# Two layers of a hybrid decoder trunk: weight and activation tiles moved to other SBUF addresses

## The chip, the core and the metric

The kernel runs on one core of one Trainium2 chip. The time is device microseconds of one execution, and the number compared is the median of three executions. The profile is of one further execution, and its records give the start and length of every instruction on TensorE (PE for its matmuls, PEld for its weight loads), VectorE (DVE), ScalarE (ACT), GpSimd (POOL) and of the DMA transfers that SyncE (SP) issues.

## What is computed

The reference is a decoder trunk with two layers over 256 tokens of width 1024, all in float32. Each layer is, cut to its matrix products:

```python
for i in range(DEPTH):                       # DEPTH = 2
    h = rms_norm(x, mix_norm_g[i])
    z = h @ w_in[i]                          # 1024 -> 4608: q, k, v, ssm, conv, three gates
    y_attn = sliding_window_attention(...) @ w_attn_out[i]
    y_ssm = glu(gelu(s5_ssm(...)) @ w_ssm_glu[i] + b_ssm_glu[i])
    y_conv = conformer_conv(...)             # ends in @ w_pw_out
    merged = gates[0] * y_attn + gates[1] * y_ssm + gates[2] * y_conv
    x = x + merged @ w_mix_out[i]
    f_gate, f_up = split(rms_norm(x, ffn_norm_g[i]) @ w_ffn_in[i])     # 1024 -> 2 x 2816
    x = x + (silu(f_gate) * f_up) @ w_ffn_out[i]
    e = p[i] @ w_ple_in[i]
    x = x + sigmoid(rms_norm(x, ple_norm_g[i]) @ w_ple_gate[i]) * e
return rms_norm(x, final_norm_g)
```

## The kernel before

All weights are read once from HBM, as 260 pairs of blocks of 128x512 floats (`total`, line 309). A pair lands in one of three `raw` tiles (`load_w`, line 313). ScalarE rounds it to a `wh` tile in the type float32r and VectorE writes the remainder into a `wl` tile (`split`, line 229, called from `prep_w`, line 336). There are four `wh` and four `wl` tiles, 4096 bytes per partition each, all from the pool `wp` (line 88). Activations are split in the same way into a high and a low tile, from the pool `act`: the groups `b4` (4096 bytes, line 92) and `b2` (2048 bytes, line 95).

`gemm` (line 462) forms a product as three float32r matmuls, high by high, high by low and low by high. The stationary operand is 128 columns of an activation tile (512 bytes per partition) and the moving operand is 512 columns of a weight tile (2048 bytes per partition):

```python
mm(acc[t], hi, wh[:, kk, :], k == 0, False)
mm(acc[t], hi, wl[:, kk, :], False, False)
mm(acc[t], lo, wh[:, kk, :], False, last)
```

One pair of blocks serves two token halves and two k, so 12 such matmuls. The last four pairs are the exception: `last_gate` (line 1369) uses them 512 columns wide for the first token half and in two parts of 256 columns for the second. Gate and GLU products end in a bias matmul whose moving operand is a `brow` tile and whose stationary operand is `sdT` (for gates, line 1161) or `ones` (for the GLU, line 1203): 24 and 16 of them. So there are 3,072 + 24 + 40 = 3,136 matmuls of 512 float32r columns in the products, and 12 more that write the attention mask. The last pair of weights has its split tiles in `b4` (lines 340 to 342, named `whl` and `wll`), not in `wp`.

The order of all instructions is written by hand: a planner in Python (`run`, line 122, `may_run`, line 403, `pump`, line 417) keeps a modelled clock per engine and decides after each half pair which piece of side work is emitted. For it, a 512-column float32r matmul costs 0.4167 ns a column plus `PE_SET`, 13.3 ns (lines 44 and 225). The planner keys its tiles by name and by offset inside the tile; it knows no SBUF address.

Tiles get their addresses in the order in which the pools are opened and in which each tile or tag is first asked for: first `cp` (constants, `x0`, `x1`, tables), then `wp` (`raw`, `wh`, `wl`), then `act`, which begins with the statistics tiles `nst` (128 bytes each, `norm_stats`, line 490) and goes on with `b4`, `b1`, the small tiles and `b2`. A tile that grows ahead of them therefore moves everything behind it.

Of the kernel before, what the change touches and what calls it, by code (L numbers as in the profile page):

```python
# [6 lines left out]
F32 = mybir.dt.float32  # L7
# [9 lines left out]
NT = 2  # L17
# [64 lines left out]
def trunk_kernel(tc, wts, par, bmat, cst_d, x_d, pos_d, pt_d, bias_d, fg_d, out_d, dbg=None):  # L82
# [3 lines left out]
    with ctx:  # L86
        cp = ctx.enter_context(tc.tile_pool(name="cp", bufs=1))
        wp = ctx.enter_context(tc.tile_pool(name="wp", bufs=5))
        act = ctx.enter_context(tc.tile_pool(name="act", bufs=2))
# [158 lines left out]
                dbg(nc, name, ap)  # L248

        cst = cp.tile([128, C_MASK], F32, name="cst")  # L250
        xs = [cp.tile([128, D], F32, name=f"x{t}") for t in range(NT)]
        pos = cp.tile([128, NT], I32, name="pos")
        pars = [cst[:, C_PAR:C_MASK], cp.tile([128, N_PA], F32, name="par1")]
# [234 lines left out]
                    pump(slack)  # L488

        def norm_stats():  # L490
            return act.tile([128, 16, NT], F32, tag="nst", bufs=5, name="nst")

        def stat(sts, i, t):
            return sts[:, i, t:t + 1]
# [601 lines left out]
        def layer(l, feat, sts, prep):  # L1096
# [156 lines left out]
            mT.upto(2)  # L1253

            fst = norm_stats()
            fT = []

# [52 lines left out]
            def hid_lhs(t, k):  # L1310
                while len(hid) <= k // 2:
                    push()
                return hid[k // 2][0][:, t, k % 2, :], hid[k // 2][1][:, t, k % 2, :]

            pst = norm_stats()
            gT = []
            for n in range(2):
# [16 lines left out]
            gT[0].upto(2)  # L1334

            nst = norm_stats()
            nT = []

# [311 lines left out]
```

## Time and profile before

| | before |
|---|---|
| median of three runs | 862.08 us (859.58 to 862.19) |
| the profiled execution's own time | 860.29 us |
| span of its profile | 858.5 us |
| mean granted TensorE clock | 0.994 |
| PE busy | 840.4 us, 98% |
| DVE, ACT, POOL busy | 68%, 53%, 15% |
| DMA | 141.34 MB, mean 165 GB/s |

Matmuls overlap in the records: one starts before the one ahead of it has ended. The length of a record is therefore no price. The step from one start to the next is, and so is the length of a piece of the chain divided by the matmuls in it.

### The profile page before, as it was taken

To read this page: it belongs to the slowest core of one execution; us is meant where nothing else is said; L and a number is where in the kernel's file an instruction comes from. 1 tells how busy PE (TensorE), PEld (TensorE's weight loads), DVE (VectorE), ACT (ScalarE), POOL (GpSimd) and SP (SyncE) were. 2 spreads that over 40 slices of the span, in tenths; PEclk is the share of its full clock that TensorE was granted. 3 is DMA by queue.
4 is the path that set the end of the run, shared out by engine and by line. 5 is a ranking of instruction groups with operands and counts; after the bars stand their busy time and mean duration, and the time that the engine had idled before them with its cause. 6 is when DMAs were issued, how large, how long until landed. Compare 5 with 4: busy or idle time off the path is not lost.

```text
span 858.5 us, 11139 instructions
## 1 busy us (share of the span) xinstructions
PE 840.4 (98%) x3976; PEld 686.8 (80%) x3976; DVE 580.9 (68%) x865; ACT 457.2 (53%) x745; POOL 126.8 (15%) x325
## 2 busy tenths in 40 slices
PE   8989999899999999999999999999999999999996
PEld 7877788688888888888888878878888888888885
DVE  4688875887667784654577599568766666654555
ACT  5675756345556666543564554544554454444454
POOL 5787001000744200000020000100000000000001
PEclk9999999989999999999999999999999999999999
DMA  7554533436765654666654443655566666666661
GB/s 252 181 178 138 152 120 98 123 99 180 211 173 177 187 177 148 179 182 190 184 152 145 124 123 101 191 174 173 172 185 180 182 177 187 181 179 189 182 185 75
DMA packets 41199, 141.34 MB, mean 165 GB/s; under 512 B 4756, under 2 KB 6404, under 8 KB 41144
## 3 DMA queue, kind: packets, MB, share of 16 engines
q1 hardware_dynamic: 41144, 140.64, 55.2%
q8 instruction: 31, 0.51, 0.2%
q14 instruction: 24, 0.20, 0.1%
HBM read 139.49 MB, written 1.13 MB: 164 GB/s over the span
## 4 chain that ended last, share of the span: by engine, by line
PE 88%; ACT 4%; DVE 3%; DMA 2%; POOL 1%; issue 1%; SPq 0%; POOLq 0%; ACTq 0%; DVEq 0%
PE fz L227 29%; PE g L227 15%; PE fo L227 14%; PE mo L227 5%; PE pz L227 4%; PE yg L227 3%; DMA raw<-in_wts 2%; PE ya L227 2%; PE sc L227 2%; PE pl L227 1%; PE zq L227 1%; PE ez L227 1%; PE zc L227 1%; PE yc L227 1%; PE yx L227 1%; ACT wh L176 1%
## 5 line engine op out<-in xcount | busy, mean ns | idle before, releaser
L200 DVE TENSOR_TENSOR wl<-raw,wh 128x1024 fp32r<-128x1024 f32 (+1 forms) x261 | 316.2, 1215 | 212.5 <-ACT wh L176 212.4
L176 ACT CAST wh<-raw 128x1024 fp32r<-128x1024 f32 (+1 forms) x261 | 271.6, 1043 | 205.2 <-PE fo L227 57.0
L200 POOL TENSOR_TENSOR nst<-nst 128x2 f32<-128x2 f32 (+1 forms) x14 | 2.8, 199 | 538.9 <-ACT sqj L171 538.4
L227 PE MATMUL fz<-wh,f0h 128*128 128x512 f32 x176 | 70.9, 403 | 0.0
L227 PE MATMUL fz<-wh,f1h 128*128 128x512 f32 x176 | 70.4, 400 | 0.0
L227 PE MATMUL fo<-wh,hdh 128*128 128x512 f32 x176 | 69.8, 397 | 0.0
L227 PE MATMUL fz<-wh,f1l 128*128 128x512 f32 x176 | 69.6, 395 | 0.0
L227 PE MATMUL fz<-wh,f0l 128*128 128x512 f32 x176 | 69.5, 395 | 0.0
L227 PE MATMUL fo<-wh,hdl 128*128 128x512 f32 x176 | 69.5, 395 | 0.0
L227 PE MATMUL fo<-wl,hdh 128*128 128x512 f32 x176 | 69.5, 395 | 0.0
L227 PE MATMUL fz<-wl,f1h 128*128 128x512 f32 x176 | 69.5, 395 | 0.0
L227 PE MATMUL fz<-wl,f0h 128*128 128x512 f32 x176 | 69.4, 394 | 0.0
L227 PEld LDWEIGHTS fo<-wh,hdl 128*128 128x128 f32 x176 | 33.1, 188 | 7.9
L227 PEld LDWEIGHTS fz<-wh,f1l 128*128 128x128 f32 x176 | 33.1, 188 | 7.9
L227 PEld LDWEIGHTS fz<-wh,f0l 128*128 128x128 f32 x176 | 33.1, 188 | 7.8
L227 PEld LDWEIGHTS fo<-wh,hdh 128*128 128x128 f32 x176 | 33.1, 188 | 7.7
L227 PE MATMUL g<-wh,h1h 128*128 128x512 f32 x96 | 38.7, 403 | 0.6 <-DVE M L210 0.6
L227 PEld LDWEIGHTS fo<-wl,hdh 128*128 128x128 f32 x176 | 33.1, 188 | 7.6
L227 PEld LDWEIGHTS fz<-wl,f1h 128*128 128x128 f32 x176 | 33.1, 188 | 7.5
L227 PEld LDWEIGHTS fz<-wh,f1h 128*128 128x128 f32 x176 | 33.1, 188 | 7.4
L227 PE MATMUL g<-wh,h0h 128*128 128x512 f32 x96 | 39.0, 406 | 0.0
L227 PEld LDWEIGHTS fz<-wl,f0h 128*128 128x128 f32 x176 | 33.2, 188 | 7.2
(390 smaller groups left out, 1766.6 us busy)
## 6 DMA issues: line engine op xcount, KB each, us to landing
raw<-in_wts SPq DMA_DIRECT2D x258, 512.0 KB
raw<-in_wts SPq DMA_DIRECT2D x4, 256.0 KB
out<-e SPq DMA_DIRECT2D x4, 256.0 KB
x<-in_x SPq DMA_DIRECT2D x4, 128.0 KB
x<-in_x SPq DMA_DIRECT2D x2, 256.0 KB
bm<-in_bmat SPq DMA_DIRECT2D x4, 128.0 KB
pT<-in_pt SPq DMA_DIRECT2D x2, 256.0 KB
fgb<-in_fg SPq DMA_DIRECT2D x1, 512.0 KB
```

The costliest lines, as they stand in the source:

```text
L176: ACT.copy(out=out, in_=in_)
L200: (eng or DVE).tensor_tensor(out=out, in0=a, in1=b, op=op)
L227: PE.matmul(out, lhsT, rhs, start=start, stop=stop)
```

## The change

One tile that nothing uses, of 40 floats (160 bytes), is asked for behind `cst`, and the statistics tiles are six instead of five (128 bytes more).

```diff
         cst = cp.tile([128, C_MASK], F32, name="cst")
+        cp.tile([128, 40], F32, name="pad")
         xs = [cp.tile([128, D], F32, name=f"x{t}") for t in range(NT)]
@@
         def norm_stats():
-            return act.tile([128, 16, NT], F32, tag="nst", bufs=5, name="nst")
+            return act.tile([128, 16, NT], F32, tag="nst", bufs=6, name="nst")
```

The instructions of every engine, their order and what they wait for stand as before; only addresses differ. Everything in `cp` behind `cst` and all of `wp` moves by 160 bytes, and everything in `act` behind `nst` by 288 bytes. The start within a partition, as the remainder by 1024 and by 512:

| tiles | mod 1024 before | after | mod 512 before | after |
|---|---|---|---|---|
| `raw`, `wh`, `wl` | 864 | 0 | 352 | 0 |
| `b4`, `b1`, `b2`: activations high and low, `whl`, `wll` | 480 or 992 | 256 or 768 | 480 | 256 |
| `x0`, `x1` | 704 | 864 | 192 | 352 |
| `brow` | 384 | 544 | 384 | 32 |
| `sdT` | 384 | 544 | 384 | 32 |
| `ones` | 384 | 32 | 384 | 32 |
| `cst` (with the identity of the transposes) | 128 | 128 | 128 | 128 |

Offsets inside a tile are multiples of 512 bytes for the stationary operands and of 2048 bytes for the moving ones (1024 in the parts of 256 columns), so the column by 512 holds for each operand that a matmul reads.

## Rows read from the trace of the kernel before

**Rows 1.** The page: busy time of the engines, and the granted clock.
```profile
PE 840.4 (98%) x3976; PEld 686.8 (80%) x3976; DVE 580.9 (68%) x865; ACT 457.2 (53%) x745; POOL 126.8 (15%) x325
...
PEclk9999999989999999999999999999999999999999
```
**Rows 2.** The page: the chain that ended last, by engine.
```profile
PE 88%; ACT 4%; DVE 3%; DMA 2%; POOL 1%; issue 1%; SPq 0%; POOLq 0%; ACTq 0%; DVEq 0%
```
**Rows 3.** What PE waited for: us in total, times, longest.
```profile
PE sT L307 <- DVE gtm L214: 3.2, 1, 3.2
PE h0p L307 <- DMA x<-in_x: 1.5, 2, 0.9
PE sc L227 <- ACT qT L171: 1.5, 1, 1.5
```
**Rows 4.** The chain in order of time: start us, us, what.
```profile
10.22 5.71 DMA raw<-in_wts
33.65 5.12 DMA raw<-in_wts
...
265.31 11.20 PE fz L227 x48
...
352.11 29.39 PE fo L227 x126
382.37 29.27 PE fo L227 x126
```
**Rows 5.** Busy time of each engine in three of those pieces.
```profile
265.31:276.51 11.20, 11.20 (x50) 8.97 (x50) 6.84 (x11) 10.14 (x15) 6.84 (x28) 1.00 0.56 172
352.11:381.50 29.39, 29.39 (x129) 23.62 (x128) 14.13 (x13) 12.20 (x15) 0.00 (x0) 1.00 0.63 184
```
**Rows 6.** PE in order of time, inside the first FFN product: start us, us.
```profile
303.07 0.39 PE L227 MATMUL fz<-wl,f0h 128*128 128x512 f32 x1
303.30 0.40 PE L227 MATMUL fz<-wh,f0l 128*128 128x512 f32 x1
303.54 0.39 PE L227 MATMUL fz<-wh,f0h 128*128 128x512 f32 x1
303.76 0.40 PE L227 MATMUL fz<-wl,f0h 128*128 128x512 f32 x1
304.00 0.39 PE L227 MATMUL fz<-wh,f0l 128*128 128x512 f32 x1
304.23 0.40 PE L227 MATMUL fz<-wh,f0h 128*128 128x512 f32 x1
304.47 0.39 PE L227 MATMUL fz<-wl,f0h 128*128 128x512 f32 x1
304.70 0.40 PE L227 MATMUL fz<-wh,f0l 128*128 128x512 f32 x1
304.94 0.39 PE L227 MATMUL fz<-wh,f0h 128*128 128x512 f32 x1
```
**Rows 7.** PEld in order of time, the same stretch.
```profile
303.07 0.19 PEld L227 LDWEIGHTS fz<-wh,f0l 128*128 128x128 f32 x1
303.30 0.19 PEld L227 LDWEIGHTS fz<-wh,f0h 128*128 128x128 f32 x1
```
[...]
**Rows 9.** PE in order of time, the last product: parts of 256 columns.
```profile
845.33 0.28 PE L227 MATMUL pl<-wh,p1h 128*128 128x256 f32 x1
...
847.49 0.28 PE L227 MATMUL pl<-whl,p1h 128*128 128x256 f32 x1
...
848.20 0.28 PE L227 MATMUL pl<-wh,p1h 128*128 128x256 f32 x1
```
**Rows 10.** PE in order of time, around a bias matmul.
```profile
587.99 0.40 PE L227 MATMUL yg<-wh,sTl 128*128 128x512 f32 x1
588.22 0.39 PE L227 MATMUL yg<-brow,ones 128*128 128x512 f32 x1
588.45 0.40 PE L227 MATMUL g<-wh,h1h 128*128 128x512 f32 x1
588.69 0.39 PE L227 MATMUL g<-wl,h1h 128*128 128x512 f32 x1
```
**Rows 11.** The page: the two costliest groups of ACT and DVE.
```profile
L200 DVE TENSOR_TENSOR wl<-raw,wh 128x1024 fp32r<-128x1024 f32 (+1 forms) x261 | 316.2, 1215 | 212.5 <-ACT wh L176 212.4
L176 ACT CAST wh<-raw 128x1024 fp32r<-128x1024 f32 (+1 forms) x261 | 271.6, 1043 | 205.2 <-PE fo L227 57.0
```

## Prediction, made before the changed kernel was run

> **What bounds the kernel now.** I read the busy shares first: PE is busy for 98% of the span, at the full granted clock, and every other engine is far below it [rows 1]. The chain of waits agrees, 88% of it is PE [rows 2]. PE's own waits are then seen to be small: the longest entry is 3.2 us, the next two 1.5 us each [rows 3]. So the time is the number of PE's instructions by their spacing, and a change that alters no instruction can act in one place above all: the spacing.
>
> The spacing is read from the chain in order of time. A piece of 126 float32r matmuls of 512 columns takes 29.39 us, which is 233.3 ns each, and the next such piece 29.27 us, 232.3 ns each; a piece of 48 takes 11.20 us, 233.3 ns each [rows 4]. I take 232.8 ns. 3,136 such matmuls at 232.8 ns are 730 us of the 858.5 us span.
>
> [...]
>
> The steps are also not equal. Between nine starts they are 0.23, 0.24, 0.22, 0.24, 0.23, 0.24, 0.23 and 0.24 us [rows 6]: the four short ones add to 0.91 us, 228 ns each, and the four long ones to 0.96 us, 240 ns each. The operands' addresses are the same modulo 512 in all of them, and the alternation does not follow the cycle of three products. It looks like two readers, the moving stream and the weight load, that get in each other's way more or less by how they happen to be in step. That reading is an inference from the spacing; no row names it.
>
> **The change, part by part.** Nothing is removed or added but two tiles; the order on every engine and all waits stay, so there is no new wait, no queue that is moved past and no DMA more. What is left is the price of each access at its new address.
>
> *Matmuls.* The moving operand goes from 352 to 0 modulo 512 and the stationary one from 480 to 256, so the distance between them goes from 128 to 256 bytes. No row has this pair of positions, so I bound it. [...] Above: if every step became a long one of 240 ns, 7.2 ns more, 22.6 us more. In between, if every step became a short one of 228 ns, 4.8 ns less, 15.1 us less. No change at all is zero. I take the short step. The reason is that it is a value which the same operands already reach in every second step, so it needs only a more favourable phase and no new speed; and the planner's own price for this matmul, 213.3 + 13.3 = 226.7 ns, is near it and 6 ns below what this layout shows. That is weak evidence, and I say so in the chances.
>
> *Casts and subtractions.* They read `raw` and write `wh` and `wl`, all moved: 261 at 1,043 ns on ACT and 261 at 1,215 ns on DVE [rows 11]. Both engines are idle for over 200 us in front of these groups, so a price that differed by 5% either way (52 and 61 ns) would be hidden by the tiles prepared ahead. Only at the start, where PE waits for them, does it show; there a dozen tiles matter, under 1 us either way. I take zero.
>
> *DMA.* `raw` rows of 4096 bytes begin 32 bytes past a multiple of 64 before and on one after. The chain holds two longer stretches of weight loading, 5.71 and 5.12 us [rows 4], inside its 2% of DMA [rows 2]. If the landing became 5% faster or slower, that is 0.5 us. I take zero. If PE becomes faster, more of the chain turns into DMA in the mixing stages, but DMA is busy for 0.56 to 0.63 in the dense stretches [rows 5] and a step shorter by 2% asks for 2% more of it.
>
> *Transposes and small products.* The identity does not move, and the rest of the span beside the 730 us is some 128 us; 2% of that would be 2.6 us. I take zero.
>
> Sum: 860.3 (the profiled execution) less 15.1 is 845.2 us. The median of the runs lies 1.8 us above the profiled execution, so the forecast for the median is **847 us**.
>
> [...] Rows 5 show that neighbours don't slow PE; what they can't show is whether PE's own two streams do. [...]
>
> **The rivals.**
>
> *No effect.* [...] For it: two other positions already occur and hardly differ. The moving operand is a `brow` tile at 384 with a neighbouring weight load of `ones`, and the steps around it are 0.23, 0.23 and 0.24 us [rows 10]; the last pair of weights lies at 480, level with its stationary operands, and its six narrow matmuls take 0.71 us, 118 ns each, against 120 ns from `wp` [rows 9]. Against it: each of these is a handful of matmuls in the middle of a pattern, and 1 to 2 ns is all that would be needed. Within 0.3% (about what a measurement of this kernel can tell from no change, 2.6 us or 0.8 ns a step) the time is 862 us.
>
> *Slower: the long step locks in.* Moving and stationary operands now both begin on multiples of 256. If being level at that scale makes the two readers meet more often rather than less, the long step becomes the rule: 860.3 + 22.6 + 1.8 is 885 us with every step at 240 ns, and half of that, 873 us, if it shifts the mix by half. It decides from 233.6 ns a step on. For it: the long step exists in every second place. Against it: no row shows two long steps in a row.
>
> [...]
>
> **How the numbers follow.** Forecast and its neighbourhood, a step between 226 and 232 ns: 0.42. No effect: 0.29. Slower: 0.21. All or most of the extra time gone: 0.08. Faster is the first and the last, 0.50. The predicted time is the forecast's, 847 us. The range is to leave out 0.2: from below the case in which most goes, 0.08 and a little of the forecast's own lower end, which puts the low end at 826 us (a step of about 221 ns); from above the larger half of the slower case, which puts the high end at 868 us (a step of 234.7 ns). Faster and no effect hold most of the chance; the forecast's own range is 839 to 858 us (steps of 225.5 to 231.5 ns).
>
> **What would show it.** Right: the two pieces of 126 matmuls of the FFN's second product shrink from 29.39 and 29.27 us to about 28.7 us, the starts of rows 6 are all 0.23 us apart, PE stays at 98% and the chain keeps its shape. No effect: the same pieces within 0.1 us. Slower: they go to 30 us or more with steps of 0.24 us in a row. Wrong in another way: equal steps and yet another time, which would put the effect on DMA, ACT or DVE, seen in rows 11 and in PE's waits.

## The result and the profile after

The changed kernel takes 846.85 us (median of four executions, 846.34 to 847.78). The kernel before takes 862.13 us in the same comparison. The ratio is 0.9831 with a 95% interval of 0.981 to 0.9851: faster by 1.7%, and the forecast was 847 us. The profiled execution took 846.71 us with a span of 844.9 us. Of the 15.3 us between the two medians, the granted clock may account for a part. In the comparisons of the experiments, 26 executions of the kernel before with a mean granted clock of 0.994 or 0.995 took 859.8 us on average, and 25 with 0.990 to 0.992 took 861.8 us; all four executions of the changed kernel had 0.993 or 0.994, and those of the kernel before beside them have no clock on record. The two profiled executions, both at 0.994, differ by 13.6 us (860.29 and 846.71). (In one run below, with the activations 96 bytes lower, the profiled execution had a granted clock of 0.556; it is left out, and the ratio given there rests on the other nine.)

First the page: busy shares, and the chain by engine.

```profile
PE 825.7 (98%) x3976; PEld 683.9 (81%) x3976; DVE 580.7 (69%) x865; ACT 458.2 (54%) x745; POOL 129.6 (15%) x325
...
PE 92%; ACT 3%; DVE 1%; DMA 1%; issue 1%; POOL 1%; SPq 1%; POOLq 0%; ACTq 0%; DVEq 0%
...
L200 DVE TENSOR_TENSOR wl<-raw,wh 128x1024 fp32r<-128x1024 f32 (+1 forms) x261 | 316.4, 1215 | 206.1 <-ACT wh L176 203.8
L176 ACT CAST wh<-raw 128x1024 fp32r<-128x1024 f32 (+1 forms) x261 | 272.6, 1046 | 199.1 <-PE fo L227 55.6
```

PE is as full as it was [rows 1] and has 14.7 us less to do with the same 3,976 records; outside its busy time the span has 19.2 us where it had 18.1. PE's part of the chain is 92% where it was 88% [rows 2]. The cast and the subtraction cost what they cost before, 1,046 against 1,043 ns and 1,215 against 1,215 [rows 11], although the tiles they read and write have moved too. So the new addresses change neither price.

The chain in order of time, the pieces that answer to [rows 4] (start us, us, what):

```profile
262.46 10.94 PE fz L227 x48
...
347.75 28.61 PE fo L227 x126
377.23 28.59 PE fo L227 x126
```

126 matmuls take 28.61 and 28.59 us where they took 29.39 and 29.27, and 48 take 10.94 where they took 11.20. That is 227.1, 226.9 and 227.9 ns a step instead of 233.3, 232.3 and 233.3. The two pieces of 126, which differed by 0.12 us before, are now alike. The gain is spread over the whole span, as a price per matmul must be. Read from the starts of the same pieces in both traces, the first long piece of the first FFN begins 1.84 us earlier (215.62 for 217.46), that of its second product 4.36 us earlier (347.75 for 352.11). In the second layer the same two pieces begin 8.78 us (624.70 for 633.48) and 11.60 us earlier (751.16 for 762.76), and the span ends 13.6 us earlier.

PE in order of time inside the second FFN product, in the stretch where nothing interrupts it (start us, length us):

```profile
359.65 0.39 PE L227 MATMUL fo<-wh,hdl 128*128 128x512 f32 x1
359.88 0.39 PE L227 MATMUL fo<-wh,hdh 128*128 128x512 f32 x1
360.10 0.39 PE L227 MATMUL fo<-wl,hdh 128*128 128x512 f32 x1
360.33 0.39 PE L227 MATMUL fo<-wh,hdl 128*128 128x512 f32 x1
360.56 0.39 PE L227 MATMUL fo<-wh,hdh 128*128 128x512 f32 x1
...
361.92 0.39 PE L227 MATMUL fo<-wh,hdh 128*128 128x512 f32 x1
362.14 0.39 PE L227 MATMUL fo<-wl,hdh 128*128 128x512 f32 x1
```

Eleven steps from 359.65 to 362.14 are 2.49 us, 226.4 ns each, and none is a long one: the alternation of 0.23 and 0.24 us of [rows 6] is gone. It takes a while to get there. Behind four transposes, in the first FFN product:

```profile
298.02 0.40 PE L227 MATMUL fz<-wl,f0h 128*128 128x512 f32 x1
298.26 0.40 PE L227 MATMUL fz<-wh,f0l 128*128 128x512 f32 x1
298.49 0.40 PE L227 MATMUL fz<-wh,f0h 128*128 128x512 f32 x1
298.73 0.39 PE L227 MATMUL fz<-wl,f0h 128*128 128x512 f32 x1
298.95 0.39 PE L227 MATMUL fz<-wh,f0l 128*128 128x512 f32 x1
299.18 0.40 PE L227 MATMUL fz<-wh,f0h 128*128 128x512 f32 x1
299.42 0.39 PE L227 MATMUL fz<-wl,f0h 128*128 128x512 f32 x1
299.64 0.40 PE L227 MATMUL fz<-wh,f0l 128*128 128x512 f32 x1
299.88 0.39 PE L227 MATMUL fz<-wh,f0h 128*128 128x512 f32 x1
300.11 0.39 PE L227 MATMUL fz<-wl,f0h 128*128 128x512 f32 x1
```

The nine steps from 298.02 to 300.11 take 2.09 us, 232.2 ns each, with 0.24 us still among them. After that the steps stay at 227. So this break of the stream by transposes costs some 50 ns behind it; over all such breaks the mean is 36 ns (see e9).

### The profile page after: what moved, and what is told of

Read it like the earlier page. It is cut to its first block, busy times and chain, and to the rows that moved or that the text cites. A ratio compares the mean times of both kernels' runs of the same rounds, so it can differ in the third digit from the quotient of the medians.

```text
span 844.9 us, 11139 instructions
## 1 busy us (share of the span) xinstructions
PE 825.7 (98%) x3976; PEld 683.9 (81%) x3976; DVE 580.7 (69%) x865; ACT 458.2 (54%) x745; POOL 129.6 (15%) x325
## 4 chain that ended last, share of the span: by engine, by line
PE 92%; ACT 3%; DVE 1%; DMA 1%; issue 1%; POOL 1%; SPq 1%; POOLq 0%; ACTq 0%; DVEq 0%
PE fz L227 29%; PE g L227 16%; PE fo L227 14%; PE mo L227 5%; PE pz L227 4%; PE yg L227 3%; PE zq L227 3%; PE zc L227 2%; PE sc L227 2%; PE ya L227 2%; PE pl L227 1%; PE ez L227 1%; PE yc L227 1%; PE yx L227 1%; PE po L227 1%; PE hT L308 1%
## 5 line engine op out<-in xcount | busy, mean ns | idle before, releaser
L200 DVE TENSOR_TENSOR wl<-raw,wh 128x1024 fp32r<-128x1024 f32 (+1 forms) x261 | 316.4, 1215 | 206.1 <-ACT wh L176 203.8
L176 ACT CAST wh<-raw 128x1024 fp32r<-128x1024 f32 (+1 forms) x261 | 272.6, 1046 | 199.1 <-PE fo L227 55.6
```

The lines of the kernel that those rows point to most:

```text
L176: ACT.copy(out=out, in_=in_)
L200: (eng or DVE).tensor_tensor(out=out, in0=a, in1=b, op=op)
```

## Experiments

Distance means: start of the stationary operand less start of the moving operand, in bytes, modulo 256. It is 128 in the kernel before (480 less 352) and 0 in the changed one (256 less 0).

### Which part of the change does it: e1 and e2

The change moves two groups of tiles. Each run makes one of the two moves alone. Theory D says that only the distance counts, theory A that each operand's own alignment does, theory W that aligned writes of the weight tiles do.

Run e1, the pad alone:

```diff
         cst = cp.tile([128, C_MASK], F32, name="cst")
+        cp.tile([128, 40], F32, name="pad")
```

> The pad alone: weight tiles at 0 modulo 512 (before: 352), activation tiles at 128 (before: 480). The distance from the moving to the stationary start stays 128 as in the kernel before. Theory D (the distance between the two operands decides, not where each lies): no gain, steps of about 232.8 ns, about 862 us. Theory A (each operand's own alignment decides): the weights have theirs, the activations don't, so about half of the gain, 852 to 857 us. Theory W (what counts is that the loads, casts and subtractions write aligned weight tiles): the whole gain, about 847 us.

Run e2, the sixth statistics tile alone:

```diff
-            return act.tile([128, 16, NT], F32, tag="nst", bufs=5, name="nst")
+            return act.tile([128, 16, NT], F32, tag="nst", bufs=6, name="nst")
```

> The sixth statistics tile alone: weight tiles stay at 352 modulo 512, activation tiles come to 96. The distance is 256 as in the changed kernel, but neither operand begins on a multiple of 64. Theory D (distance): the whole gain, steps of about 227 ns, 846 to 849 us. Theory A (own alignment): no gain, about 862 us. Theory W (aligned writes of the weight tiles): no gain, about 862 us.

Measured: e1 has a ratio to the kernel before of 0.9991 (0.998 to 1.0001), 860.37 us; e2 has 0.9841 (0.9825 to 0.9858), 846.99 us. The chain of e1, its two pieces of 126:

```profile
350.81 29.29 PE fo L227 x126
380.97 29.28 PE fo L227 x126
```

and of e2:

```profile
350.46 28.59 PE fo L227 x126
379.92 28.59 PE fo L227 x126
```

In e1 the weight tiles begin on multiples of 1024 as in the changed kernel, and nothing is gained. In e2 neither operand begins on a multiple of 64 (352 and 96 modulo 512), and the whole gain is there. Theories A and W fall in both runs and D holds in both: what counts is where the two operands lie to each other. Which stationary operand it is, the matmul's own or the next one's, these two runs can't tell, as all activation tiles move together; e8 asks that.

### Other distances: e3, e4, e5, e6, e7, e10, e11

All have the pad, so weights lie at 0 modulo 512; the activations are moved by the number of statistics tiles and, from e5 on, by a small unused tile ahead of them.

Run e3, activations at 0 modulo 512 (two of four buffers of small attention statistics pay for the room):

```diff
-            return act.tile([128, 16, NT], F32, tag="nst", bufs=6, name="nst")
+            return act.tile([128, 16, NT], F32, tag="nst", bufs=8, name="nst")
...
-            st = act.tile([128, 6, 8], F32, tag="ast", bufs=4, name="ast")
+            st = act.tile([128, 6, 8], F32, tag="ast", bufs=2, name="ast")
```

> Pad and eight statistics tiles: weights and activations both at 0 modulo 512, distance 0 (two of four small attention statistics tiles are given up for the room; they are long done when they come again). Theory D: another distance, so another step than 226.7 ns; the nearest row, the last pair of weights at distance 0 in the kernel before, speaks for about 232 to 233 ns, 858 to 864 us. Theory A: both aligned at least as well as in the changed kernel, 845 to 848 us. Theory W: about 847 us.

Run e4, activations at 384:

```diff
-            return act.tile([128, 16, NT], F32, tag="nst", bufs=6, name="nst")
+            return act.tile([128, 16, NT], F32, tag="nst", bufs=7, name="nst")
```

> Pad and seven statistics tiles: weights at 0 modulo 512, activations at 384, distance 384. Theory D: 384 is as far from 256 as 128 is, on the other side; if the step depends on how far the distance is from 256, about 232 ns and 858 to 863 us; if only on the order of the two, something between 840 and 862 us. Theory A: activations on a multiple of 128 and not of 256, 850 to 857 us. Theory W: about 847 us.

Run e5, 64 bytes more than in the changed kernel:

```diff
+        act.tile([128, 16], F32, tag="pd", bufs=1, name="pd")
+
         def norm_stats():
```

> The changed kernel with 64 bytes more ahead of the activation tiles: the stationary start lies 64 bytes above the moving start, modulo 256 (changed kernel: 0, kernel before: 128). Theory G (the step grows with how far the distance is from a multiple of 256): half way between the two, steps of about 229.7 ns, 852 to 856 us. Theory P (only a multiple of 256 is good, any other distance is alike): as before, about 232.5 ns, 859 to 862 us. Theory L (a coarse level: distances under 128 are alike): as the changed kernel, 226.7 ns, 846 to 849 us.

Run e6, 64 bytes less:

```diff
+        act.tile([128, 16], F32, tag="pd", bufs=1, name="pd")
+
         def norm_stats():
-            return act.tile([128, 16, NT], F32, tag="nst", bufs=6, name="nst")
+            return act.tile([128, 16, NT], F32, tag="nst", bufs=5, name="nst")
```

> The changed kernel with 64 bytes less ahead of the activation tiles: the stationary start lies 64 bytes below the moving start, modulo 256 (192 above). Theory G (grows with the distance from a multiple of 256 on either side): 852 to 856 us, equal to the run with 64 above. Theory P: 859 to 862 us. Theory L: 859 to 862 us, as the distance is over 128. If what counts is which of the two reads first, the two runs with 64 bytes differ, and one of them may lie under 846 us.

Run e7 is e5 with `[128, 8]`, 32 bytes more than in the changed kernel:

> The changed kernel with 32 bytes more ahead of the activation tiles: stationary 32 bytes above moving, modulo 256. Theory G: a quarter of the way back, about 228.2 ns, 849 to 852 us. Theory P: 859 to 862 us. Theory L: 846 to 849 us.

Runs e10 and e11 are e6 with `[128, 24]` and `[128, 8]`, 32 and 96 bytes less than in the changed kernel:

> The changed kernel with the activation tiles 32 bytes lower: stationary 32 bytes below moving, modulo 256 (distance 224). So far: 0 gives 226.7 ns a step, 32 and 64 give 233.2, 128 gives 232.8, 192 gives 228.9. Theory U (uneven slope: below a multiple of 256 the price rises gently, above it at once): between 226.7 and 228.9 ns, 846 to 850 us. Theory V (no slope: each distance settles in a pattern of its own, and only 0 is exact): anywhere up to 233.5 ns, 850 to 863 us.

> The changed kernel with the activation tiles 96 bytes lower: stationary 96 bytes below moving, modulo 256 (distance 160). Theory U (gentle rise below a multiple of 256): between 228.9 and 232.8 ns, 852 to 860 us. Theory V (a pattern of its own at each distance): not bound to lie between, up to 863 us.

Measured, by distance modulo 256. The step is the first piece of 126 matmuls of the chain divided by 126; for e11 none is given:

| distance | run | weights, activations mod 512 | ratio to before | 95% interval | step, ns |
|---|---|---|---|---|---|
| 0 | the changed kernel | 0, 256 | 0.9831 | 0.981 to 0.9851 | 227.1 |
| 0 | e2 | 352, 96 | 0.9841 | 0.9825 to 0.9858 | 226.9 |
| 0 | e3 | 0, 0 | 0.9852 | 0.9836 to 0.9869 | 227.1 |
| 32 | e7 | 0, 288 | 1.0021 | 1.0011 to 1.0032 | 233.3 |
| 64 | e5 | 0, 320 | 1.0027 | 1.0016 to 1.0038 | 233.3 |
| 128 | the kernel before | 352, 480 | 1 | | 233.3 |
| 128 | e1 | 0, 128 | 0.9991 | 0.998 to 1.0001 | 232.5 |
| 128 | e4 | 0, 384 | 0.9987 | 0.9977 to 0.9997 | 232.5 |
| 160 | e11 | 0, 160 | 1.0023 | 1.0009 to 1.0037 | |
| 192 | e6 | 0, 192 | 0.9889 | 0.987 to 0.9908 | 228.9 |
| 224 | e10 | 0, 224 | 1.001 | 0.9997 to 1.0023 | 233.4 |

The rows of the chain behind them, in the order e3, e4, e5, e7:

```profile
350.48 28.61 PE fo L227 x126
...
351.43 29.29 PE fo L227 x126
...
352.10 29.39 PE fo L227 x126
...
351.99 29.39 PE fo L227 x126
```

e6:

```profile
349.02 28.84 PE fo L227 x126
378.74 28.85 PE fo L227 x126
```

and e10:

```profile
355.56 29.41 PE fo L227 x126
385.84 29.40 PE fo L227 x126
```

Three things follow. The pattern has a period of 256: e3 at 0 modulo 512 is as good as the changed kernel at 256, which theory D had expected to be different (858 to 864 us; 848.53 measured), and e4 at 384 is as bad as e1 at 128. Of the distances tried, only 0 gives the whole gain: 32 bytes off on either side costs all of it, so theory G's slope and theory L's coarse level both miss. P is right that e5 and e7 gain nothing, although 863.19 and 862.50 us lie a little above its 859 to 862. But P misses e6, which 64 bytes below keeps two thirds of the gain (850.54 us, inside no range but near G's and under L's and P's). The order of the two starts alone does not explain e6 either: the runs 64 bytes above and below differ, as that reading has it, but those 32 bytes above and below do not (862.50 and 861.91 us). Between e6 and 0 lies e10 with no gain, so U's gentle rise below a multiple of 256 is out as well, in both of its runs (861.91 and 863.53 us). V, which only says that each distance settles in a pattern of its own, is what is left. It forbids little, and e11 lies 0.5 us above its 863. Why 192 is a good one is open.

### Which two operands meet: e8

In the changed kernel the bias rows and their stationary operands were left at 32 modulo 512. PE in order of time around one bias matmul of the changed kernel:

```profile
574.63 0.39 PE L227 MATMUL yg<-wh,sTh 128*128 128x512 f32 x1
574.85 0.39 PE L227 MATMUL yg<-wl,sTh 128*128 128x512 f32 x1
575.08 0.40 PE L227 MATMUL yg<-wh,sTl 128*128 128x512 f32 x1
575.32 0.39 PE L227 MATMUL yg<-brow,ones 128*128 128x512 f32 x1
575.55 0.39 PE L227 MATMUL yg<-wh,sTh 128*128 128x512 f32 x1
575.78 0.40 PE L227 MATMUL yg<-wl,sTh 128*128 128x512 f32 x1
576.01 0.39 PE L227 MATMUL yg<-wh,sTl 128*128 128x512 f32 x1
```

The step turns long, 0.24 us from 575.08 to 575.32, one matmul ahead of the bias matmul. That matmul reads `wh` and `sTl` at distance 0; what is off is the weight load of `ones` for the next one, which in PEld's records starts with it at 575.08 us and runs beside it for 0.19 us. The bias matmul's own two operands lie at 32 both, distance 0, so a rule of each matmul's own pair would leave no long step here. Run e8 takes the changed kernel and splits its padding so that these tiles lie at 0 modulo 256 as well:

```diff
-        cp.tile([128, 40], F32, name="pad")
...
+        cp.tile([128, 32], F32, name="pad")
         ones = cp.tile([128, 128], F32R, name="ones")
...
+        cp.tile([128, 8], F32, name="pad2")
         ubuf = cp.tile([128, 2, 30 + 256], F32, name="ubuf")
```

> The changed kernel with the same 160 bytes of padding in two parts, 128 ahead of the ones tile and 32 behind the bias rows, so that the bias rows, their stationary operands and the mask lie at distance 0 too (in the changed kernel 32 modulo 512 against 256). Weights and activations as in the changed kernel. In the changed kernel a bias matmul is followed by five steps of 230 to 235 ns before 226.7 returns, about 27 ns in all, by 40 bias matmuls. Theory D (distance of whatever two operands meet): those steps go, about 1 us less, 845 to 847 us, and no step over 228 ns after a bias matmul in the trace. A rival, that the bias matmul's steps come from its being the last of its group: the same steps stay and the time is the changed kernel's, 846 to 848 us.

The same place in e8:

```profile
576.46 0.39 PE L227 MATMUL yg<-wh,sTh 128*128 128x512 f32 x1
576.68 0.39 PE L227 MATMUL yg<-wl,sTh 128*128 128x512 f32 x1
576.91 0.39 PE L227 MATMUL yg<-wh,sTl 128*128 128x512 f32 x1
577.14 0.39 PE L227 MATMUL yg<-brow,ones 128*128 128x512 f32 x1
577.37 0.39 PE L227 MATMUL yg<-wh,sTh 128*128 128x512 f32 x1
577.59 0.39 PE L227 MATMUL yg<-wl,sTh 128*128 128x512 f32 x1
577.82 0.39 PE L227 MATMUL yg<-wh,sTl 128*128 128x512 f32 x1
```

The six steps take 1.36 us, 226.7 ns each, against 1.38 us, 230.0 ns each, in the changed kernel, and no long one is among them. Over the 40 bias matmuls of the gates and the GLU, but for one or two that stand beside a break, the step ahead of the bias matmul is 235 ns on average in the changed kernel and 227 ns in e8. That the bias matmul is the last of its group, the rival, is therefore not the cause: it still is. In the whole comparison e8 has 0.9828 (0.9808 to 0.9848), 846.64 us, against 0.9831 for the changed kernel. The 1 us expected is smaller than the intervals, so the trace shows it and the time can't.

### The way back after a break: e9

```diff
+        cp.tile([128, 32], F32, name="pad")
         cst = cp.tile([128, C_MASK], F32, name="cst")
...
-        cp.tile([128, 32], F32, name="pad")
         ones = cp.tile([128, 128], F32R, name="ones")
```

(against e8)

> The version with the bias rows at distance 0, and its 128 bytes of padding ahead of the constants instead, so that the identity of the transposes begins on a multiple of 256 too (before: 128 above one). After each break by a transpose the changed kernel's steps need some ten matmuls to come back to 226.7 ns, about 32 to 36 ns in all a time, some 80 times, 2 to 3 us. Theory I (the way back is long because the transposes' operands lie at another distance): it shortens, up to 2 us less, 844 to 846 us. Rival (the way back depends on how the weight load and the stream happen to start, not on where the identity lies): no change, 846 to 847 us.

Measured: 0.9831 (0.9805 to 0.9856), 846.88 us. With the identity on a multiple of 256 the way back costs about the same as in e8. Over the eleven steps that follow the first, long one behind a break, the time above 226.7 ns a step is 36 ns in the changed kernel, 32 ns in e8 and 30 ns in e9, each a mean over 47 or 48 breaks that scatter by 11 to 17 ns. The rival holds. No version here beats the changed kernel by more than the intervals.

## Why the prediction was right

*That only the spacing can move.* Right. PE's share, its longest waits (3.2 and 1.5 us in both traces) and the length of casts and subtractions are as before, and the difference is found in the steps of the float32r matmuls.

*That the step is set by two readers, the moving stream and the weight load of the next matmul.* It was an inference from the alternation. The runs bear it out as far as addresses go: e1 (a ratio of 0.9991) and e2 (0.9841) show that the relative position decides and not where either lies, and the step ahead of the bias matmuls, 235 ns in the changed kernel and 227 ns in e8, shows that the partner of a stream is the stationary operand of the next matmul. No record shows what the two do to each other, so that they get in each other's way stays the author's inference. ACT and POOL do not set the step ([rows 5], and in the changed kernel 227.9 ns a step with ACT busy for 10.16 of 10.94 us and POOL for 6.61, against 227.1 ns with ACT busy for 12.15 of 28.61 us and POOL for nothing). With equal instructions it is 226.7 or 233 ns by address alone.

*The size.* The term was 4.8 ns by 3,136 matmuls, 15.1 us. In the long pieces the steps fell by 5.4 to 6.2 ns, somewhat more than taken (227 instead of 228 ns). The span fell by 13.6 us, less than 5.4 by 3,136 (16.9 us): each break and each bias matmul is followed by steps that are still long, which the prediction had not counted, and PE's time outside its busy time grew by 1.1 us. So the term was 1.5 us too large for the profiled executions. The 1.8 us added for the median were too much as well: the changed kernel's median lies 0.1 us above its profiled execution. The two errors cancel, so that 847 met 846.85 this closely is luck; the gain itself was sized to about a tenth.

*Why the short step.* The reason given, that the operands reach it already in every second step, pointed the right way, but the new step is not the old short one. In starts read to the nanosecond, which the trace holds, the steps of [rows 6] are 229 or 230 and 237 or 238 ns in turn; the 228 ns of the prediction came from starts rounded to 10 ns. The changed kernel's settled steps are 226 or 227 ns, and of the 518 steps in the second FFN products of the kernel before only two are under 228 ns. So the distance did not lock the stream into its short step; it gave it a shorter one. The planner's constant of 226.7 ns turned out to be the price at distance 0, which does not show where the constant came from.

*The case in which most of the extra time goes.* Its chance of 0.08 and the low end of 826 us (a step of about 221 ns) were the author's estimate: no run shows how long a step without that time would be, nor a stretch at 221 ns. The shortest steps that hold over a stretch are those at distance 0, 226.4 ns over the eleven above.

*Wide and narrow matmuls.* In the changed kernel a matmul of 512 columns takes 226.7 ns and one of 256 columns 120 ns (in the chain the last product's 24 wide and 48 narrow matmuls take 11.20 us, which is 24 at 226.7 and 48 at 120). The 106.7 ns between the two are 0.4167 ns a column, the planner's figure, and by it 13.3 ns, its `PE_SET`, are left at either width. It is tempting to call these 13.3 ns a fixed price and the 6 ns more of the kernel before what the distance adds, but e5, at distance 64, speaks against it. Two of its narrow matmuls, 13 steps apart:

```profile
849.58 0.28 PE L227 MATMUL pl<-wh,p1l 128*128 128x256 f32 x1
...
851.05 0.28 PE L227 MATMUL pl<-whl,p1h 128*128 128x256 f32 x1
```

That is 1.47 us, 113 ns a step, where the wide matmuls of the same run take 233.3 ns: 120 ns between the two widths instead of 106.7. So the step depends on distance and width together, and what the 13.3 ns are is open.

*The rivals.* No effect rested on two other positions seen in the trace before. They were too few matmuls in the middle of a pattern, as the prediction noted. The last pair of weights there was at distance 0, the very best, and its narrow matmuls at 118 ns could not tell, because a narrow one gains nothing from that distance (118 to 120 ns before, 120 ns in the changed kernel). The pair's six wide matmuls, which the prediction did not look at, could not tell either. The first of them:

```profile
843.93 0.40 PE L227 MATMUL pl<-whl,p1h 128*128 128x512 f32 x1
```

From there to the first narrow one at 845.33 [rows 9] are 1.40 us, 233 ns each. Six are fewer than the ten or so that the stream needs to settle behind a break in the changed kernel.

Slower needed 233.6 ns a step or more; the distance with the highest ratio, 64, comes to 233.3 ns and a ratio of 1.0027, and the longest step, at 224, is 233.4 ns, so no distance tried came near the end at 885 us.

## What to carry to other kernels

When TensorE is full (98% here) and its float32r matmuls of 512 columns with 128-column weights start more than 226.7 ns apart, look at the distance between the moving operand and the stationary operand of the next matmul: here a multiple of 256 bytes gave 226.7 ns, 192 gave 228.9, and 32, 64, 128 and 224 gave 232.5 to 233.4. For 256 columns it gave nothing: 120 ns, where distance 64 had a stretch at 113 (e5). Aligning one of the two tiles did nothing by itself (e1, a ratio of 0.9991). An edit that adds or removes a small tile ahead of large ones can change this (e7, one tile of 32 bytes: 862.50 us for 846.85), so compare the step before and after, not only the total.

## What the runs showed that was not expected

- The step depends on the distance modulo 256 bytes and not smoothly: 0 gives 226.7 ns, 192 gives 228.9 ns, and 32, 64, 128 and 224 give 232.5 to 233.4 ns.
- At distance 0 the stream needs about ten matmuls to settle behind a break by transposes: in the changed kernel nine steps of 230.6 ns on average over 48 breaks (232.2 ns in the one shown) before 227 holds.
- At distance 0 a matmul takes 226.7 ns at 512 columns and 120 ns at 256; at distance 64 it takes 233.3 ns at 512 and, in a stretch of narrow ones, 113 ns at 256.
